# Attention on normalised queries and keys, one core: other homes for the second pair's squares and the early roots, a last pair in three pieces, values loaded one pair later, and new order lists

## The chip, the core and the metric

The kernel runs on one core of one Trainium2 chip. A core has a matrix engine (PE in the profile, with its weight loads as PEld), VectorE (DVE), ScalarE (ACT), GpSimd (POOL) and a sync engine (SP) that issues most transfers. The matrix engine writes its results into the accumulation memory PSUM; everything else lives in the on-chip memory SBUF. The metric is device time in microseconds (us) of one launch; lower is better.

## What is computed

Queries and keys are scaled to length one, their products divided by tau = 0.1, and a softmax over the keys weighs the values. There are 8 x 12 = 96 heads of 512 positions and 64 dimensions.

```python
Q_norm = Q / (np.linalg.norm(Q, axis=-1, keepdims=True) + 1e-10)
K_norm = K / (np.linalg.norm(K, axis=-1, keepdims=True) + 1e-10)
scores = np.einsum('bhqd,bhkd->bhqk', Q_norm, K_norm) / tau
weights = np.exp(scores - np.max(scores, axis=-1, keepdims=True))
weights = weights / (np.sum(weights, axis=-1, keepdims=True) + 1e-10)
return np.einsum('bhqk,bhkd->bhqd', weights, V)
```

Scores lie between -10 and 10 here, so the kernel takes the exponential without the maximum. The row sum comes from a column of ones beside the values.

## The kernel before

The 96 heads are worked off as 48 pairs, s = 0 to 47. One pair passes through these operations; the names in capitals are the keys that the code gives them, and w is 0 for queries and 1 for keys.

- **LD, LV** (L286, L289, L292): SP loads Q, K and V of the pair, 256 KB each. For pair 0, Q and K come in halves of 128 KB, the K halves issued by ACT.
- **SQ** (L227, L229, L306, L308, L313): squares of Q and K. From pair 3 on POOL squares both in one instruction of 128x1024. In pair 1, DVE squares Q (L308) and ACT squares K (L306); in pair 2, ACT squares Q and POOL squares K.
- **SSQ, RED** (L330, L337, L341): sums of squares. Either PE adds eight slices into PSUM with eight products against the identity (SSQ) and DVE finishes the sum (RED, L337), or DVE sums straight from SBUF (L341).
- **LOG, NEW** (L355, L357, L360): one over the root. For pairs 1, 2 and 3 ACT takes a logarithm (LOG) into `ys` and then exp(-x/2) (NEW, kind 7) into `xs` in SBUF, and DVE copies that to PSUM (`nps`, L360; NEW, kind 6). From pair 4 on DVE takes Newton steps. For pair 0 it is done by halves (L236, L240, called NRMS).
- **SCL** (L246, L389): Q and K times their roots, into `qn`. Q is on DVE; K is on POOL, but on DVE for the pairs in `K_ON_DVE` (1, 2, 3, 4, 9, ...).
- **TR, EVA** (L254, L395, L402): PE transposes `qn` into PSUM, DVE copies it out to `qt`.
- **SCO, EXP** (L429, L445): for each of four blocks c of 128 keys PE makes the scores of both heads in `scps`, and ACT writes their exponential to `et`, 128x1024 in one instruction. `scps` holds two such blocks; SCO of block c waits for EXP of block c-2.
- **VC** (L450): POOL turns the values into bf16.
- **PV, RCP, NRM, ST** (L459, L474, L476, L483): PE multiplies `et` with the values, head 0 into bank `ops0` and head 1 into `ops1`; DVE takes one over the row sum (RCP) and scales into `ob` (NRM); SP stores.

In the last pair, 47, block c = 3 is taken by two instructions of 128x512, one for each head, and each head has its own RCP, NRM and store of 128 KB.

The engines run side by side and meet only at semaphores. Nothing is decided at run time: `ORDER` (L525) holds one list per engine, and each engine issues its operations in the order of its list, waiting before each for what it needs (`write`, L67). An operation that waits therefore holds up all that stands behind it on its engine. The PE list also holds fill products on zeros (L188). The first part of the lists, by names:

```
PE   ... TR(0,K,h0) TR(0,Q,h0) SSQ(1,Q) fill TR(0,K,h1) fill fill SSQ(1,K) fill SCO(0,c1,h0) TR(0,Q,h1)
     SCO(0,c0,h0) SSQ(2,Q) SCO(0,c0,h1) SCO(0,c1,h1) SSQ(2,K) SCO(0,c2) TR(1,K) TR(1,Q) SCO(0,c3) SCO(1,c0) ...
ACT  ... NRMS(0,K,h1) NRMS(0,Q,h1) SQ(1,K) SQ(2,Q) LOG(1) EXP(0,c1,h0) NEW(1) EXP(0,c0,h0) EXP(0,c0,h1)
     EXP(0,c1,h1) LOG(2) NEW(2) EXP(0,c2) EXP(0,c3) EXP(1,c0) LOG(3) NEW(3) EXP(1,c1) ... (EXP only from here)
DVE  ... SCL(0,Q,h0) SQ(1,Q) EVA(0,K,h0) EVA(0,Q,h0) RED(1,Q) SCL(0,Q,h1) RED(1,K) EVA(0,K,h1) EVA(0,Q,h1)
     copy(1) RED(2,Q) SCL(1,K) RED(2,K) SCL(1,Q) copy(2) EVA(1) SCL(2,K) SCL(2,Q) RED(3) RED(3) copy(3) EVA(2) ...
```

Of the kernel before, what the change touches and what calls it, by code (L numbers as in the profile page):

```python
# [3 lines left out]
ALU = mybir.AluOpType  # L4
# [102 lines left out]
def bass_cosine_similarity_attention_kernel(  # L107
# [162 lines left out]
    def new(g):  # L270
        if g <= 0:
            return []
        return [("NEW", g, k) for k in (6, 7)]

    def pair(s):
# [6 lines left out]
        for w, x in ((0, Q), (1, K)):  # L282
            if s == 0:
                for h in range(2):
                    P.add(("LD", 0, w, h), "act" if w else "sp", "ldh", -1000 + h,  [],
                          lambda e, w=w, x=x, h=h: e.dma_start(out=qk[iq][:, w, h], in_=src(x, s)[:, h]), slot=f"head{w}_{h}")  # L286
                continue
            P.add(("LD", s, w), "sp", "ld1" if s == 1 else "ld", s, [*([("SCL", 0, w, 0), ("SCL", 0, w, 1), ("SQ", 0, w, 0), ("SQ", 0, w, 1)] if s == R_QK else [key("SCL", s - R_QK, w), key("SQ", s - R_QK, w if s - R_QK in SQ_ON else 0)])],
                  lambda e, w=w, x=x: e.dma_start(out=qk[iq][:, w], in_=src(x, s)),  # L289
                  slot=f"first{s}_{w}" if s <= 2 else f"qk{iq}")  # L290
# [9 lines left out]
        elif s in SQ_ON:  # L300
            for w, eng in enumerate(SQ_ON[s]):
                half, dst = qk[iq][:, w], sq[iqs][:, 8 * w : 8 * w + 8, :]
                half = half.rearrange("p h x -> p (h x)")
                dst = dst.rearrange("p g d -> p (g d)")
                if eng == "act":
                    emit = lambda e, half=half, dst=dst: e.activation(out=dst, in_=half, func=ACT.Square)  # L306
                else:
                    emit = lambda e, half=half, dst=dst: e.tensor_tensor(out=dst, in0=half, in1=half, op=ALU.mult)  # L308
                P.add(("SQ", s, w), eng, {"act": "sqa", "dve": "sqv", "pool": "sqp"}[eng],
                      due_sq(s) + 0.1 * w, [("LD", s, w)] + red[w] + (["table"] if eng == "act" else []), emit)  # L310
        else:
            P.add(("SQ", s, 0), "pool", "sq", due_sq(s), [("LD", s, 0), ("LD", s, 1)] + reds_,
                  lambda e: e.tensor_tensor(out=sqf, in0=data, in1=data, op=ALU.mult))  # L313
# [8 lines left out]
        for w in range(2):  # L322
            sqs = ("SQ", s, w if s in SQ_ON else 0)
            dst = x2[:, w, c8 : c8 + 8]
            if (s, w) in session:
# [9 lines left out]
                P.add(("SSQ", s, w), "pe", "ssq", due, [sqs, "eye"] + before, ssq)  # L335
                P.add(("RED", s, w), "dve", "redp", due + 0.1, [("SSQ", s, w), ("NRMS", 0, 0, 1), *new(g - R_X)],
                      lambda e, bank=bank, dst=dst: e.tensor_reduce(  # L337
                          out=dst, in_=o_ps[bank][:, 320:384].rearrange("p (g e) -> p g e", e=8), axis=AX.X, op=ALU.add))
            else:
                P.add(("RED", s, w), "dve", "red", due_red(s) + 0.5 * w, [sqs, ("NRMS", 0, 0, 1), *new(g - R_X)],  # L340
# [11 lines left out]
        if s == first[g] and g in NORM_ON_ACT:  # L352
# [3 lines left out]
            P.add(("NEW", g, 7), "act", "sm_act", at + 0.01, [("LOG", g)],  # L356
                  lambda e: e.activation(  # L357
                      out=xs[g][:, 0 : 2 * m], in_=ys[g % R_X][:, 0 : 2 * m], func=ACT.Exp, scale=-0.5)).own = True
            P.add(("NEW", g, 6), "dve", "new", TF - 2.6, [("NEW", g, 7), ("NRMS", 0, 0, 1)],
                  lambda e: e.tensor_copy(out=n_ps[:, g % R_X, 128 : 128 + 2 * m], in_=xs[g][:, 0 : 2 * m]))  # L360
# [22 lines left out]
        for w in range(2):  # L383
# [4 lines left out]
                  [("NEW", g, 6 if acts and dve else 6 + w + (dve and w))] + ([("TR", 0, w, 0), ("TR", 0, w, 1)] if s == R_QN else [key("TR", s - R_QN, w)]),  # L388
# [23 lines left out]
    def exps(s, c):  # L412
        if s < 0:
            return []
        if s == NP - 1 and c == NT - 1 or s == 0 and c < 2:
# [3 lines left out]
    def rest(s):  # L419
# [3 lines left out]
        for c in range(NT):  # L423
# [15 lines left out]
            for hs in ((0,), (1,)) if s == 0 and c < 2 or last_pair and c == NT - 1 else ((0, 1),):  # L439
# [13 lines left out]
                  scalar1=1.0, scalar2=1.0, op0=ALU.mult, op1=ALU.mult))  # L453
        for h in range(2):
            for i in range(NT):
                def pv(e, h=h, i=i):
                    for k in range(NT):
                        t, c = (k, i) if last_pair else (i, k)
# [3 lines left out]
                            start=(c == 0 and (t == 0 or not last_pair)), stop=(c == NT - 1),  # L462
                            skip_group_check=last_pair)
# [3 lines left out]
                if last_pair:  # L467
                    need = [("EXP", s, i, h) if i == NT - 1 else ("EXP", s, i)]
                    due = T0 + 0.9 * i + 2.5 + 0.1 * h
# [9 lines left out]
        for h in range(2) if last_pair else (None,):  # L479
            hs = slice(0, 2) if h is None else slice(h, h + 1)  # L480
            P.add(("ST", s) if h is None else ("ST", s, h), "sp", "ld", s + STORE_AT,
                  [("NRM", s, i) for i in range(hs.start, hs.stop)],
                  lambda e, hs=hs: e.dma_start(  # L483
                      out=src(out, s)[:, hs], in_=ob[io][:, hs].rearrange("p h t d -> p h (t d)")),
                  slot=f"out{io}" if h is None else f"outz{h}")
# [6 lines left out]

GROUPS = [1, 1, 1, 1, 2]
SQ_ON = {1: ("dve", "act"), 2: ("act", "pool")}
# [6 lines left out]
VLAG = 3  # L501
# [19 lines left out]
def slack(s, most):  # L521
# [5 lines left out]
        "7 8 64 65 103 104 11 142 143 66 180 181 105 223 224 144 257 258 182 299 300 225 333 334 259 376 377 301 410 "  # L527
        "411 335 452 453 63 378 102 412 141 454 179 222 486 487 528 529 562 563 488 605 606 530 639 640 256 564 681 682 "
        "298 607 715 716 332 641 757 758 375 683 791 792 409 717 834 835 451 759 868 869 485 793 910 911 527 836 944 "
        "945 561 870 986 987 604 912 1020 1021 638 946 1063 1064 680 988 1097 1098 714 1022 1139 1140 756 1065 1173 "  # L530
        "1174 790 1099 1215 1216 833 1141 1249 1250 867 1175 1292 1293 909 1217 1326 1327 943 1251 1368 1369 985 1294 "
        "1402 1403 1019 1328 1444 1445 1062 1370 1478 1479 1096 1404 1521 1522 1138 1446 1555 1556 1172 1480 1597 1598 "
        "1214 1523 1631 1632 1248 1557 1673 1674 1291 1599 1707 1708 1325 1633 1749 1750 1367 1675 1783 1784 1401 1709 "
        "1825 1826 1443 1751 1477 1785 1520 1827 1554 1596 1630 1672 1706 1748 1782 1824 1859 1860 "
    ),
    "pool": (
        "0 1 2 4 14 27 22 35 107 50 145 89 183 226 128 260 209 166 302 232 336 379 243 274 285 308 319 413 396 438 351 "
        "455 362 472 489 531 427 461 565 608 642 503 591 514 537 684 718 580 548 760 794 837 656 625 690 667 871 913 "
        "701 732 766 743 777 947 854 809 820 989 1023 1066 1100 885 930 919 896 1142 1176 961 1006 972 995 1083 1159 "
        "1049 1218 1038 1125 1252 1295 1329 1114 1148 1371 1278 1312 1405 1190 1201 1235 1224 1354 1447 1267 1388 1481 "  # L540
        "1524 1558 1343 1507 1377 1430 1541 1600 1634 1419 1464 1583 1453 1676 1617 1496 1710 1659 1752 1693 1786 1572 "
        "1606 1735 1828 1769 1811 1648 1682 1846 1724 1758 1800 1834 "
    ),
    "dve": (
        "5 13 15 26 28 19 67 24 21 70 32 72 37 34 75 109 78 111 76 114 80 117 115 147 149 152 119 155 184 153 55 186 56 "
        "227 229 61 187 62 188 189 157 190 191 192 100 263 193 194 101 195 196 198 261 200 94 303 305 95 264 139 265 "
        "230 266 140 267 133 234 268 134 269 177 271 270 380 171 339 172 272 337 276 178 382 214 340 306 341 215 342 "
        "220 343 221 344 310 345 347 346 414 349 348 248 416 249 385 353 456 254 458 383 417 255 418 290 419 291 420 "
        "387 421 296 422 297 423 424 425 459 324 492 325 330 490 331 429 532 367 534 368 493 566 494 373 495 374 496 "
        "463 497 609 498 568 401 500 499 402 407 501 408 643 505 535 611 443 569 444 570 449 571 450 572 539 573 685 "  # L550
        "574 477 645 575 576 478 578 577 719 614 483 582 612 687 519 646 484 647 520 648 616 649 761 650 525 651 526 "
        "653 652 553 721 554 654 559 688 795 658 763 560 596 722 838 723 597 724 602 725 603 726 692 727 872 729 630 "
        "797 728 631 730 636 914 764 637 840 734 798 799 678 800 672 801 679 802 673 803 805 804 768 806 712 807 713 "
        "706 874 707 841 948 811 843 990 916 748 875 749 876 877 1024 878 754 879 755 845 880 950 881 882 782 883 783 "
        "788 917 1101 789 887 1067 825 992 826 951 952 831 953 832 954 921 955 956 957 1026 958 859 959 865 860 866 "
        "1177 1143 963 993 901 1069 902 1027 907 1028 908 1029 1030 1031 1032 997 1033 1034 1036 1035 935 1103 936 1070 "
# [90 lines left out]
```

## Time and profile before

| | |
|---|---|
| four runs | 191.6, 191.83, 191.97, 192.09 us; median 191.9 us |
| the profiled execution | 191.83 us, of which the profile's span is 190.1 us |
| granted PE clock in it | 1.0 |
| busy share of the span | PE 93%, ACT 96%, DVE 89%, POOL 81% |
| EXP, all sizes (L445, ACT) | 195 instructions, 176.6 us busy |
| squares from pair 3 on (L313, POOL) | 45 instructions, 84.6 us busy |
| DMA | 267 GB/s mean; 256 KB loads of V land 5.0 us (median) after their issue |

The busy shares are means over three stages with different limits: a head up to the first exponential, a long body, and an end. A busy PE counts overlapping pipelined products. The useful views are the chain of work that ended last, which names at each moment what everything else waited for, and the timeline of one engine, whose last bracket says how long the engine idled before a group of instructions and what ended that. In a timeline a start stamp can lie before the end of the instruction ahead of it, as instructions overlap in the engine's pipe. The prediction shows the lines it rests on.

### The profile page before, as it was taken

The numbers are of one execution on the slowest core, as the hardware profiler recorded it, in microseconds if no ns is written. First come the engines' busy times: TensorE is split into PE (matmuls) and PEld (weight loads), VectorE is DVE, ScalarE is ACT, GpSimd is POOL, SyncE is SP. The second block draws the span as 40 slices with busy tenths as digits, with TensorE's granted clock in tenths as the row PEclk, the third lists the DMA queues.
The fourth block names the chain that finished last, engine by engine and source line by source line (L and its number), as shares of the span: only waits on it lengthen the run. The fifth ranks groups of instructions, "written<-read, shape, count | busy, mean of one in ns | idle before, by whom it ended". The sixth has DMA issues, their size and how long they took to land.

```text
span 190.1 us, 6749 instructions
## 1 busy us (share of the span) xinstructions
PE 176.4 (93%) x2730; PEld 110.8 (58%) x2730; DVE 169.0 (89%) x588; ACT 182.0 (96%) x212; POOL 154.3 (81%) x143
## 2 busy tenths in 40 slices
PE   7889999999999999999999999999999999999983
PEld 2546655656565666656566566665656555655552
DVE  2798999999999999999989999999999888968643
ACT  4599999999999999999999999999999999999993
POOL 5389999999999999999999989979999987043000
PEclk9999999999999999999999999999999999999999
DMA  5999997799999999998798896999699684222133
GB/s 151 356 350 347 349 356 262 221 302 357 380 383 351 316 282 302 382 360 249 247 338 291 263 317 211 345 299 338 217 316 328 193 294 120 62 94 74 55 110 114
DMA packets 52302, 50.76 MB, mean 267 GB/s; under 512 B 3120, under 2 KB 52272, under 8 KB 52272
## 3 DMA queue, kind: packets, MB, share of 16 engines
q1 hardware_dynamic: 51984, 50.08, 81.1%
q8 instruction: 21, 0.34, 0.8%
q10 hardware_dynamic: 288, 0.26, 0.4%
q14 instruction: 9, 0.07, 0.1%
HBM read 37.75 MB, written 12.58 MB: 265 GB/s over the span
## 4 chain that ended last, share of the span: by engine, by line
ACT 92%; DMA 3%; PE 2%; DVE 1%; SPq 0%; ACTq 0%; issue 0%
ACT et L445 92%; DMA qk<-in_Q_dram 3%; PE ops L330 1%; PE scps L429 1%; DVE ob L476 0%; SPq L286 0%; DVE sq L308 0%; ACTq L85 0%; ACT xs L357 0%; ACT ys L355 0%; PE tps L254 0%; PE scps L254 0%; PE ops L459 0%; DVE rd L474 0%; PE scps L188 0%
## 5 line engine op out<-in xcount | busy, mean ns | idle before, releaser
L445 ACT ACTIVATE et<-scps 128x1024 bf16<-128x1024 f32 (+1 forms) x195 | 176.6, 1206 | 0.0
L313 POOL TENSOR_TENSOR sq<-qk 128x1024 bf16<-128x1024 f32 x45 | 84.6, 1893 | 4.0 <-DMA qk<-in_K_dram 3.7
L429 PE MATMUL scps<-qt 64*128 64x512 bf16 x384 | 75.5, 385 | 8.4 <-ACT et L445 2.5
L459 PE MATMUL ops<-vb,et 128*128 128x65 bf16 x1536 | 76.6, 195 | 0.2 <-ACT et L445 0.2
L459 PEld LDWEIGHTS ops<-vb,et 128*128 128x128 bf16 x1536 | 57.6, 98 | 29.6 <-issue 21.1
L389 POOL TENSOR_TENSOR qn<-qk,rk 128x512 bf16<-128x512 f32 x37 | 38.3, 1043 | 11.1 <-DVE rk L367 10.4
L476 DVE TENSOR_TENSOR ob<-ops,rd 128x256 f32<-128x256 f32 x96 | 39.8, 417 | 0.3
L389 DVE TENSOR_TENSOR qn<-qk,nps 128x512 bf16<-128x512 f32 x57 | 38.0, 673 | 0.0
L429 PEld LDWEIGHTS scps<-qt 64*128 64x128 bf16 x384 | 19.6, 93 | 27.1 <-ACT et L445 10.3
L402 DVE COPY qt<-tps 128x1024 bf16<-128x1024 bf16 x47 | 32.2, 685 | 2.6 <-PE tps L395 2.0
L395 PE MATMUL tps<-ident,qn 128*128 128x128 bf16 x376 | 33.8, 220 | 0.1
L450 POOL TENSOR_SCALAR vb<-vf 128x512 bf16<-128x512 f32 x48 | 29.6, 626 | 1.4 <-PE scps L429 1.2
L341 DVE TENSOR_REDUCE nps<-sq 128x8 f32<-128x512 bf16 x44 | 29.8, 680 | 0.0
L395 PEld LDWEIGHTS tps<-ident,qn 128*128 128x128 bf16 x376 | 21.5, 98 | 11.7 <-issue 6.1
L474 DVE RECIPROCAL rd<-ops 128x4 f32<-128x4 f32 x96 | 16.8, 176 | 8.2 <-PE ops L459 5.4
L330 PE MATMUL ops<-sq,ident 128*128 128x64 bf16 x400 | 19.8, 193 | 0.7 <-DVE sq L308 0.7
L330 PEld LDWEIGHTS ops<-sq,ident 128*128 128x128 bf16 x400 | 14.9, 98 | 3.3 <-issue 1.6
L337 DVE TENSOR_REDUCE nps<-ops 128x8 f32<-128x64 f32 x44 | 9.4, 214 | 0.7 <-PE ops L330 0.6
L362 DVE TENSOR_TENSOR nps<-nps,ys 128x32 f32<-128x32 f32 x44 | 8.5, 192 | 0.4
L363 DVE SCALAR_TENSOR_TENSOR nps<-nps,ys 128x32 f32<-128x32 f32 x44 | 8.5, 192 | 0.4
L367 DVE SCALAR_TENSOR_TENSOR nps<-nps,ys 128x16 f32<-128x16 f32 x29 | 5.0, 173 | 0.1
L185 PE MATMUL ops<-warm_in,ident 128*128 128x512 bf16 x8 | 3.6, 631 | 1.4 <-POOL eps L178 1.4
(43 smaller groups left out, 37.5 us busy)
## 6 DMA issues: line engine op xcount, KB each, us to landing
vf<-in_V_dram SPq DMA_DIRECT2D x48, 256.0 KB, 5.0
qk<-in_Q_dram SPq DMA_DIRECT2D x47, 256.0 KB, 4.4
qk<-in_K_dram SPq DMA_DIRECT2D x47, 256.0 KB, 5.6
out_dram<-ob SPq DMA_DIRECT2D x47, 256.0 KB, 4.2
qk<-in_K_dram ACTq DMA_DIRECT2D x2, 128.0 KB, 2.9
qk<-in_Q_dram SPq DMA_DIRECT2D x2, 128.0 KB, 2.7
out_dram<-ob SPq DMA_DIRECT2D x2, 128.0 KB, 1.7
```

What stands on the lines that cost most here:

```text
L313: lambda e: e.tensor_tensor(out=sqf, in0=data, in1=data, op=ALU.mult))
L330: last = e.matmul(out=o_ps[bank][:, 320:384], lhsT=ident[:, :], rhs=sq[iqs][:, 8 * w : 8 * w + 8, 8 * k : 8 * k + 8], start=(k == 0), stop ...
L341: lambda e, w=w, dst=dst: e.tensor_reduce(out=dst, in_=sq[iqs][:, 8 * w : 8 * w + 8, :], axis=AX.X, op=ALU.add))
L389: lambda e, w=w, r=r: e.tensor_tensor(out=qn[iqn][:, w].rearrange("p t h d -> p h t d"), in0=qk[iq][:, w].rearrange("p h (t d) -> p h t d" ...
L395: last = e.transpose(t_ps[:, w, t, :], qn[iqn][:, w, t].rearrange("p h d -> p (h d)"), ident[:, :])
L402: lambda e: e.tensor_copy(out=qt[iqt][:, :, :, :].rearrange("p w t x -> p (w t x)"), in_=t_ps[:, :, :, :].rearrange("p w t x -> p (w t x)")))
L429: last = e.matmul(out=sc_ps[:, 2 * b + h, :], lhsT=qt[iqt][64 * h : 64 * h + 64, 1, c, :], rhs=qt[iqt][64 * h : 64 * h + 64, 0, :, :], sta ...
L445: lambda e, c=c, b=b, hs=hs: e.activation(out=et[iet][:, c, hs[0] : hs[-1] + 1, :], in_=sc_ps[:, 2 * b + hs[0] : 2 * b + hs[-1] + 1, :], f ...
L450: lambda e: e.tensor_scalar(out=vb[:, iq, :, :, 0:DIM].rearrange("p c h d -> p h c d"), in0=vf[iv][:, :, :].rearrange("p h (c d) -> p h c ...
L459: last = e.matmul(out=o_ps[h][:, 65 * t : 65 * t + 65], lhsT=et[iet][:, c, h, 128 * t : 128 * t + 128], rhs=vb[:, iq, c, h, :], start=(c = ...
L474: lambda e, h=h, grid=grid: e.reciprocal(out=rd[io][:, h, :], in_=grid[:, :, DIM]))
L476: lambda e, h=h, grid=grid: e.tensor_tensor(out=ob[io][:, h], in0=grid[:, :, 0:DIM], in1=rd[io][:, h, :].unsqueeze(2).to_broadcast([128, N ...
```

## The change

1. **SQ of pair 1** leaves DVE. Q is squared by ACT (128x512); the K square is split by heads: h0 by ACT (128x256), h1 by POOL (128x256). On ACT's list the Q square stands ahead of NRMS(0,Q,h1), the K square behind it.
2. **Roots of pairs 1 to 3**: ACT's exp(-x/2) writes to `nps` in PSUM; the three DVE copies go. NEW(2) and NEW(3) now stand one EXP behind their LOG. Each NEW also waits for the SCL of the pair before, and sums of pairs 4 to 11 wait for NEW(3).
3. **Last pair**: EXP of block c = 3, PV, RCP, NRM and the store come in three pieces: head 0 whole, head 1 rows 0 and 1, head 1 rows 2 and 3 (`PIECES`). The third piece accumulates in the transposes' PSUM bank. ACT's list has the third piece ahead of the second, PE's and SP's the second ahead of the third; DVE's ends RCP, NRM of piece 1, RCP 2, RCP 3, NRM 2, NRM 3.
4. **VLAG 3 to 4**: V of a pair is loaded one pair later; on SP's list Q and K of pairs 1 to 3 are now followed by V of pair 0 (before: pairs 1 and 2).
5. **All five lists are new**. The PE list's fills differ: 256 columns ahead of SSQ(1,Q), none behind it, one of 256 ahead of SSQ(1,K) (before 256 and 128).

```diff
+    def direct_r(g):
+        return g in NORM_ON_ACT and all(i in K_ON_DVE for i in range(first[g], first[g] + sizes[g]))
...
-            P.add(("NEW", g, 7), "act", "sm_act", at + 0.01, [("LOG", g)],
+            P.add(("NEW", g, 7), "act", "sm_act", at + 0.01, [("LOG", g)] + ([("SCL", first[g] - 1, w) for w in range(2)] if direct and g > 1 else [("NRMS", 0, 0, 1), ("SCL", 0, 0, 1)]),
                   lambda e: e.activation(
-                      out=xs[g][:, 0 : 2 * m], in_=ys[g % R_X][:, 0 : 2 * m], func=ACT.Exp, scale=-0.5)).own = True
-            P.add(("NEW", g, 6), "dve", "new", TF - 2.6, [("NEW", g, 7), ("NRMS", 0, 0, 1)],
-                  lambda e: e.tensor_copy(out=n_ps[:, g % R_X, 128 : 128 + 2 * m], in_=xs[g][:, 0 : 2 * m]))
+                      out=n_ps[:, g % R_X, 128 : 128 + 2 * m] if direct else xs[g][:, 0 : 2 * m],
+                      in_=ys[g % R_X][:, 0 : 2 * m], func=ACT.Exp, scale=-0.5)).own = True
...
+            if last_pair and c == NT - 1:
+                for k, (h, lo, hi) in enumerate(PIECES):
+                    P.add(("EXP", s, c, k), "act", "exp1" if hi - lo == NT else "exph", T0 + 0.9 * c + 0.3 * k,
+                          [("SCO", s, c)] + [key("PV", s - R_ET, i, NT - 1) for i in range(2)],
+                          lambda e, c=c, b=b, h=h, q=slice(128 * lo, 128 * hi): e.activation(
+                              out=et[iet][:, c, h, q], in_=sc_ps[:, 2 * b + h, q], func=ACT.Exp, scale=inv_tau))
...
+    def last(s, T0):
+        iq, iet, io = s % R_QK, s % R_ET, s % R_O
+        spare = t_ps[:, :, :, :].rearrange("p w t x -> p (w t x)").bitcast(f32)
+        for k, (h, lo, hi) in enumerate(PIECES):
+            bank = spare if k == 2 else o_ps[h]
+            for c in range(NT):
...
+                op = P.add(("PV", s, k, c), "pe", "pv" if hi - lo == NT else "pvh", T0 + 0.9 * c + 2.5 + 0.1 * k,
+                           [("EXP", s, c, k) if c == NT - 1 else ("EXP", s, c), ("VC", s)]
+                           + (([("EVA", s)] if k == 2 else bank_free[s, h]) if c == 0 else [("PV", s, k, c - 1)]), pv)
...
+            P.add(("ST", s, k), "sp", "ldh" if hi - lo == NT else "ldq", s + STORE_AT + k, [("NRM", s, k)],
+                  lambda e, h=h, lo=lo, hi=hi: e.dma_start(
+                      out=src(out, s)[:, h, DIM * lo : DIM * hi], in_=ob[io][:, h, lo:hi].rearrange("p t d -> p (t d)")),
+                  slot=f"outz{k}")
...
+PIECES = ((0, 0, 4), (1, 0, 2), (1, 2, 4))
-SQ_ON = {1: ("dve", "act"), 2: ("act", "pool")}
+SQ_ON = {1: ("act", ("act", "pool")), 2: ("act", "pool")}
-VLAG = 3
+VLAG = 4
```

## The prediction

> **What bounds the kernel now.** I read the chain's shares first, then the chain in order of time, then the timelines of ACT, DVE and SP at both ends. The chain's shares, then its pieces (start, length, what):
>
> ```profile
> ACT 92%; DMA 3%; PE 2%; DVE 1%; SPq 0%; ACTq 0%; issue 0%
> ```
> ```profile
> 6.91 0.70 DVE sq L308
> 7.61 0.05 issue
> 7.66 0.41 PE ops L330 x8
> ...
> 10.57 1.08 ACT et L445 x2
> 11.66 0.20 ACT ys L355
> 11.86 0.02 issue
> 11.88 0.22 ACT xs L357
> 12.10 2.74 ACT et L445 x3
> ...
> 15.28 170.48 ACT et L445 x186
> ...
> 186.86 0.42 DVE ob L476
> 187.28 0.12 DVE rd L474
> 187.40 0.02 issue
> 187.42 0.42 DVE ob L476
> ```
>
> The body is 186 exponentials in a row, 170.48 / 186 = 0.917 us each, with no idle between. The change makes none shorter. It can act on the head (DVE's square of Q1, PE's list up to 10.55, LOG and NEW between exponentials) and on the end after the last exponential; in the body it can only do harm.
>
> **Head, the square.** Before, DVE idled for Q1 and then squared, which PE and DVE's own copies (EVA of pair 0) stood behind:
>
> ```profile
> 6.91 0.69 DVE L308 TENSOR_TENSOR sq<-qk 128x512 bf16<-128x512 f32 x1 [1.13 <-DMA qk<-in_Q_dram]
> 7.52 0.41 DVE L267 COPY qt<-scps 64x512 bf16<-64x512 bf16 x1
> ```
>
> - On ACT a 128x512 square takes 0.63 (the rows at 7.62 and 8.35). From the landing at 6.88 it runs 6.91 to 7.54, so SSQ(1,Q) starts at 7.60 instead of 7.66. DVE's copies move into the idle time.
> - The fill of 192 behind it goes (7.90 to 8.07): TR(0,K,h1) starts at 7.84 instead of 8.07. Of two fills one goes (0.055): PE is ready for SSQ(1,K) at 8.17 instead of 8.46.
> - SSQ(1,K) now waits for POOL too. K1 lands at 7.60; POOL starts 0.07 after a landing (9.08 to 9.15); its 128x256 square takes 0.61 (two in the row at 3.63, 1.32 long); PE follows 0.056 later: 7.60 + 0.07 + 0.61 + 0.06 = 8.34. Gain 0.12 instead of 0.29. POOL idled from 6.66 to 9.15, so its next square is not later.
> - From there PE's list is the old one up to the score that EXP(0,c0,h1) waited for: 10.57 becomes 10.45. LOG(1) does not hold it: RED(1,K) ends at 9.01, ACT's square of Q2 at 8.98 as before.
>
> **Head, the roots.** A start-to-start reading of ACT:
>
> ```profile
> 9.15 0.31 ACT L355 ACTIVATE ys<-xs,eps 128x16 f32<-128x16 f32 x1 [0.17 <-DVE xs L337]
> 9.37 0.58 ACT L445 ACTIVATE et<-scps 128x512 bf16<-128x512 f32 x1
> 9.84 0.20 ACT L357 ACTIVATE xs<-ys 128x16 f32<-128x16 f32 x1
> 9.95 1.71 ACT L445 ACTIVATE et<-scps 128x512 bf16<-128x512 f32 x3
> 11.54 0.31 ACT L355 ACTIVATE ys<-xs,eps 128x16 f32<-128x16 f32 x1
> 11.88 0.22 ACT L357 ACTIVATE xs<-ys 128x16 f32<-128x16 f32 x1
> 12.01 2.83 ACT L445 ACTIVATE et<-scps 128x1024 bf16<-128x1024 f32 x3
> ```
>
> LOG(2), NEW(2), EXP one after the other take 12.01 - 11.54 = 0.46: NEW waits for LOG's end. With an EXP between, as pair 1 already has it, they take 0.215 (9.15 to 9.37) and 0.105 (9.84 to 9.95), 0.32. Gain 0.143 for each of pairs 2 and 3, 0.29. The copies (0.11 of DVE time each) are hidden. What a root written to PSUM costs more or less than one to SBUF I take as nothing: pair 0 has both (0.21 to `xs`, 0.16 to `nps`), bounds -0.05 to +0.05 each.
>
> What is late next: with ACT earlier by 0.12 + 0.14, SCO(0,c3) ends at 12.72 - 0.12 = 12.60 and ACT is ready at 12.64, no cover left. LOG(3) needs both RED(3): EVA(1) starts at 12.44 - 0.12 = 12.32, then 0.61 and two SCL of 0.60, so they end at 14.45, ACT may start at 14.49 and is ready at 14.45: 0.04 lost. NEW(3), 0.5 later than before, feeds SCL(3) at 15.83; counted through DVE's list with its rows, EVA(3) ends at 20.47, 0.7 before SCO(3) has to be done, which takes 0.39. That hides it. The added waits hold nothing: each NEW's SCL has ended (SCL(2) at 14.2, NEW(3) at 15.6), and the sums that wait for NEW(3) stand behind SCL(3), which needs it anyway.
>
> Head: 0.12 + 0.29 - 0.04 = **0.37 gained**. Bounds: 0.25 (the square's gain lost) to 0.45 (nothing lost, POOL's 0.06 quicker).
>
> **Body.** Loads: Q and K of pair 3 land one transfer earlier (0.75 us: 9.83 to 10.58 in place of V0), V0 at 11.34 instead of 9.83, taken by POOL at 12.5 behind SQ(3); PV(0) starts at 15.28 in the old timeline. Later on SP's list V goes out behind the store of eight pairs before instead of nine, still some seven pairs ahead of its PV; the one place where POOL may meet it is rival 3. Work ahead of each point in the lists, by rows: ahead of EVA(s) DVE has 0.94 less (0.61 + 3 x 0.11), only for pair 15 0.10 more, where the trace has 1.73 between EVA(15) and its scores. PE's largest work between two score blocks falls from 0.71 to 0.59, with the block's 0.32 under 0.917. POOL is tightest at SCL(20,K): 1.26 more work ahead of it than at the first body squares, against 1.16 of old slack and a start 0.75 earlier, with the deadline 0.37 earlier: 0.28 left. Besides, a late start of ACT by up to 0.25 costs nothing: in the trace an EXP's length grows from 1.01 at 15.19 to 1.28 later, and late starts shorten the next one while ends stay 0.917 apart. I take nothing, bounds 0 (ends without idle leave nothing to gain) and +0.95 (rival 3).
>
> **End.** Here the new parts stand against each other:
>
> ```profile
> 187.31 0.34 SPq L483 DMA_DIRECT2D out_dram<-ob  x1
> ```
> ```profile
> 187.88 0.34 SPq L483 DMA_DIRECT2D out_dram<-ob  x1
> ```
> ```profile
> DMA to landing us min/median/max: 1.7/1.7/1.7
> ```
>
> - ACT: 1024 elements end 0.917 apart, 512 0.490, so 256 cost 0.28; the last exponential ends 0.06 later, at 186.81 (old clock). PE's last products follow at 186.86 and 186.93; DVE is busy with head 0's NRM until it takes the next RCP at 187.20, as before. Hidden.
> - DVE: RCP 187.20, RCP 187.30, NRM 187.42 (0.22 behind its RCP, as at 187.20). Half an NRM: 0.42 for 256 and 0.68 for 512 elements (L389) give 0.29; the second starts 0.21 later and ends at 187.93 instead of 187.85.
> - SP: the second store may go at 187.74, the third at 187.95, but one issue takes 0.345 and the next follows 0.04 later: 188.13 instead of 187.88, **0.25 late**.
> - Landing: 128 KB takes 1.72 from issue. 64 KB is not in this trace. The final transfer ran its 1024-byte packets at 47 ns, 8 on each of 16 engines; 512-byte ones between 27 (the 4-byte ones take 7 to 9, the rest by size) and 47 give 1.57 to 1.72; by 256 KB less 128 KB (2.15 - 1.72), half a step less, 1.51. I take 1.57, by the packets: 189.70 against 189.60.
>
> The Trainium skill ("DMA: Bandwidth & Descriptors", section "Anatomy of one DMA", given for GpSimd's path, while these go from SP) says that a transfer's fixed part, about 2 us, outweighs its bytes, at 436 bytes per ns. That speaks against cutting a store: 64 KB less would save 0.15, and an uncut 128 KB would take 2.3, which the measured 1.72 contradicts. By it the third store would land at 190.28; the sum goes by the rows.
>
> End: **0.10 lost**. Bounds: 0.16 gained (third store issued as soon as its data is there, landing 1.49) to 0.26 lost (1.72).
>
> **Sum.** 191.83 - 0.37 + 0.10 = 191.56 on the profiled execution. That lies 0.07 under the median, 191.9, which would become 191.63. I forecast 191.6.
>
> **Rivals.**
> 1. *The cut store pays.* For: DVE's data is ready 0.18 before SP is, and SP's issue may be shorter for half the bytes (0.372 at 256 KB, 0.345 at 128). Against: halving saved only 0.03. With 0.16 gained and 0.40 in the head: 191.3.
> 2. *The head pays little.* ACT gets ahead, and PE's and DVE's lists, without cover at 12.6 and 14.45, hold it: the square's gain and half of the roots' go. For: 0.04 of cover. Against: DVE has 0.94 less to do. 0.37 becomes 0.1: 191.85.
> 3. *Slower: a late V load holds POOL.* VC(11) now stands ahead of VC(8), VC(10), VC(9) and SQ(12); its load is issued behind ST(3), about 32.3, where it stood behind ST(2), 28.4. POOL reaches it at about 36.2. Loads landed between 2.1 and 6.4 after issue there. At 6.4, 38.7: POOL stalls 2.5, SCL(10,K) comes 1.2 past its slack (0.76 + 0.93 - 0.37 = 1.3), ACT hides 0.25: 0.95 lost, 192.5. It costs from a landing 5.5 after issue on and outweighs the rest from 5.7. Against: loads beside it, issued at 34.8, took 3.1.
>
> **Chances.** Forecast 48%, rival 1 33%, rival 2 9%, rival 3 10%. About 0.2% (0.38 us) is what a measurement of this kernel can tell from no change. Rival 1 and a little of the forecast's lower edge are faster by more: 35%; the rest of the forecast and rival 2 are within: 55%; rival 3 is slower: 10%. Range: down to both best bounds, 191.83 - 0.45 - 0.16 = 191.2, less 0.1 for the runs' spread; up to 191.83 - 0.25 + 0.26 = 191.84 and the 0.26 by which the highest run lies over the profiled one: 191.1 to 192.1. It leaves out rival 3.
>
> **What would show it.** Right: EXP(0,c0,h1) starts near 10.45; pairs 2 and 3 show LOG, EXP, NEW with starts 0.2 and 0.1 apart from what follows; a body of exponentials 0.917 apart; three issues on SP 0.39 apart, the last landing about 1.57 later. Wrong: a gap between exponentials, a POOL wait on V, or a third issue that starts when its NRM ends.

## The result, and the profile after

The changed kernel takes 191.58 us (median of 39 runs, 190.73 to 194.61) against 191.68 us for the kernel before (60 runs on the same chips, 190.72 to 193.1): ratio 0.9993, 95% interval 0.998 to 1.0005. That is no change that this measurement can tell. Four of the 39 runs, 194.03 to 194.61 us at a granted clock of 0.988 to 0.991 (the others have 0.996 or more), are left out of the ratio. The time lies where the forecast put it (191.6), but the terms do not. The profiled execution of the changed kernel took 192.59 us with a span of 190.8, so it is 0.76 slower than the one of before (191.83, span 190.1).

From the page after: the chain's shares, the group of exponentials, POOL's squares, and the last pair's stores (KB each, us from issue to landing).

```profile
ACT 86%; PE 6%; DMA 3%; POOL 2%; issue 1%; DVE 1%; SPq 0%; DVEq 0%; POOLq 0%
...
L469 ACT ACTIVATE et<-scps 128x1024 bf16<-128x1024 f32 (+1 forms) x193 | 176.0, 1210 | 0.7 <-PE scps L446 0.6
L325 POOL TENSOR_TENSOR sq<-qk 128x1024 bf16<-128x1024 f32 x45 | 84.7, 1893 | 3.0 <-DMA qk<-in_K_dram 2.9
...
out_dram<-ob SPq DMA_DIRECT2D x1, 128.0 KB, 1.7
out_dram<-ob SPq DMA_DIRECT2D x2, 64.0 KB, 1.6
```

POOL has a share of the chain now, and the exponentials have 0.7 of idle time ahead of them (the number behind the last bar), where before they had none:

```profile
L445 ACT ACTIVATE et<-scps 128x1024 bf16<-128x1024 f32 (+1 forms) x195 | 176.6, 1206 | 0.0
```

The chain in order of time (start, length, what) says where:

```profile
6.96 0.02 issue
6.98 0.63 ACT sq L317
...
8.48 0.39 PE ops L342 x8
...
10.59 1.08 ACT et L469 x2
11.68 0.19 ACT ys L367
...
15.93 78.84 ACT et L469 x86
...
100.85 1.89 POOL sq L325
102.74 1.01 POOL qn L404
103.75 0.05 issue
103.80 0.40 PE tps L410 x4
104.19 0.34 PE scps L446 x2
104.54 0.02 issue
104.56 80.78 ACT et L469 x88
```

The body is cut in two. Ahead of 104.56 the chain is no longer ACT's own but POOL's: the square of pair 32 (SQ(32)), the K scaling of pair 26 (SCL(26,K)), its transposes, its scores. The exponential at 104.56 ends 1.655 behind the one ahead of it, instead of 0.917: **a gap of 0.74**. POOL's timeline there, with the idle time and its releaser in the bracket:

```profile
97.12 1.90 POOL L325 TENSOR_TENSOR sq<-qk 128x1024 bf16<-128x1024 f32 x1
100.85 1.89 POOL L325 TENSOR_TENSOR sq<-qk 128x1024 bf16<-128x1024 f32 x1 [1.83 <-DMA qk<-in_K_dram]
102.70 1.04 POOL L404 TENSOR_TENSOR qn<-qk,rk 128x512 bf16<-128x512 f32 x1
```

POOL stood for 1.83 us before SQ(32), because K of pair 32, issued at 94.65, landed at 100.78, and SCL(26,K) stands behind it on the new list. (From 94.8 to 100.8 the chain names PE's work, whose last signal came 0.02 before the landing. In e4, below, the same wait ends 0.07 behind the landing with PE's signal 0.34 ahead of it, so the load is what POOL waited for.) The kernel before has SCL(26,K) ahead of SQ(32) and a copy of values between them; there K of pair 32 landed at 98.67 and SQ(32) began at 102.60, so it had 3.9 us to spare:

```profile
99.15 1.89 POOL L313 TENSOR_TENSOR sq<-qk 128x1024 bf16<-128x1024 f32 x1
101.00 1.04 POOL L389 TENSOR_TENSOR qn<-qk,rk 128x512 bf16<-128x512 f32 x1
102.01 0.63 POOL L450 TENSOR_SCALAR vb<-vf 128x512 bf16<-128x512 f32 x1
```

To compare executions I cut each trace into four terms and leave out when the first loads land, which differs by up to 2 us between executions (the landing of Q1 lies between 5.28 and 7.23 in the twelve traces). Term 1 runs from the landing of K1 to the start of EXP(0,c0,h1); term 2 from there to the end of EXP(1,c2), with the roots in it; term 3, the body, to the end of head 0's last exponential; term 4, the end, to the last landing. All in us:

| kernel | K1 to EXP | roots | body | end | median of runs, ratio to before (95%) |
|---|---|---|---|---|---|
| before | 2.98 | 6.53 | 169.15 | 3.34 | |
| after | 2.94 | 6.28 | 169.87 | 3.58 | 191.58, 0.9993 (0.998 to 1.0005) |
| e1 SCL(26,K) ahead of SQ(32) | 3.33 | 6.29 | 169.85 | 3.57 | 192.2, 1.0025 (1.0006 to 1.0043) |
| e2 values as before | 3.68 | 6.29 | 172.97 | 3.57 | 194.48, 1.0164 (1.0135 to 1.0192) |
| e3 two pieces | 2.94 | 6.29 | 169.13 | 3.34 | 191.5, 1.0 (0.9984 to 1.0017) |
| e4 third store on ACT | 2.94 | 6.29 | 170.19 | 3.34 | 191.31, 0.9991 (0.9969 to 1.0013) |
| e6 roots alone | 2.95 | 6.29 | 170.47 | 3.34 | 191.65, 0.9983 (0.9957 to 1.001) |
| e7 square alone | 2.94 | 6.54 | 169.15 | 3.35 | 191.74, 0.9999 (0.9975 to 1.0024) |
| e8 POOL refilled | 2.94 | 6.28 | 169.13 | 3.56 | 191.29, 0.9962 (0.9937 to 0.9988) |
| e9 roots, squares on ACT | 2.83 | 6.29 | 169.24 | 3.34 | 191.16, 0.997 (0.9949 to 0.9991) |
| e10 refilled, store on ACT | 2.94 | 6.29 | 169.13 | 3.34 | 191.18, 0.9982 (0.9965 to 0.9999) |
| e11 as e10, K1 on ACT | 2.84 | 6.29 | 169.13 | 3.35 | 191.07, 0.9962 (0.9945 to 0.9979) |

The terms come from one traced execution each, the medians and ratios from 6 to 39 runs of a kernel. Where K1 lands early (6.47 in e1, 5.98 in e2), term 1 is longer, as PE's own list then sets that start (the chain of both runs through PE alone from 1.41 to the exponential); those two say nothing of the square.

For the change as a whole: term 1 gains 0.04, term 2 gains 0.25, term 4 loses 0.24, and term 3 loses 0.72 in the traced execution. Without the gap the sum would be a gain of 0.05.

### The profile page after: what moved, and what is told of

It reads as the page before. It is cut to its first block, busy times and chain, and to the rows that moved or that the text cites. A ratio compares the mean times of both kernels' runs of the same rounds, so it can differ in the third digit from the quotient of the medians.

```text
span 190.8 us, 6749 instructions
## 1 busy us (share of the span) xinstructions
PE 177.4 (93%) x2729; PEld 110.3 (58%) x2729; DVE 167.9 (88%) x586; ACT 182.4 (96%) x214; POOL 154.9 (81%) x144
## 4 chain that ended last, share of the span: by engine, by line
ACT 86%; PE 6%; DMA 3%; POOL 2%; issue 1%; DVE 1%; SPq 0%; DVEq 0%; POOLq 0%
ACT et L469 86%; DMA qk<-in_Q_dram 3%; PE scps L446 2%; PE ops L486 1%; POOL sq L325 1%; PE ops L342 1%; PE tps L410 1%; POOL qn L404 1%; SPq L296 0%; DVE ob L527 0%; PE ops L514 0%; ACT sq L317 0%; ACT ys L367 0%; DVE rd L525 0%; PE tps L254 0%
## 5 line engine op out<-in xcount | busy, mean ns | idle before, releaser
L486 PEld LDWEIGHTS ops<-vb,et 128*128 128x128 bf16 x1504 | 56.8, 98 | 29.9 <-issue 23.8
L499 DVE TENSOR_TENSOR ob<-ops,rd 128x256 f32<-128x256 f32 x94 | 39.1, 416 | 0.4
L410 PE MATMUL tps<-ident,qn 128*128 128x128 bf16 x376 | 34.5, 220 | 1.0 <-POOL qn L404 0.9
L382 DVE SCALAR_TENSOR_TENSOR nps<-nps,ys 128x16 f32<-128x16 f32 x29 | 4.8, 173 | 0.1
```

The costliest lines, as they stand in the source:

```text
L410: last = e.transpose(t_ps[:, w, t, :], qn[iqn][:, w, t].rearrange("p h d -> p (h d)"), ident[:, :])
L486: last = e.matmul(out=o_ps[h][:, 65 * t : 65 * t + 65], lhsT=et[iet][:, c, h, 128 * t : 128 * t + 128], rhs=vb[:, iq, c, h, :], start=(c = ...
L499: lambda e, h=h, grid=grid: e.tensor_tensor(out=ob[io][:, h], in0=grid[:, :, 0:DIM], in1=rd[io][:, h, :].unsqueeze(2).to_broadcast([128, N ...
```

## The experiments

My theory after the result: the head's gain is taken back by the end, and POOL's new order makes the gap, by standing SQ(32) with a late load ahead of a scaling that is due. The rival: the values' later load makes the K loads late, whatever POOL's order.

**e1, SCL(26,K) ahead of SQ(32) again**

```diff
 POOL  ... SQ(31)
-      SQ(32) SCL(26,K) VC(29) ...
+      SCL(26,K) SQ(32) VC(29) ...
```

> One pair of entries on POOL's list changes places: the scaling SCL(26,K) stands ahead of the square SQ(32), as in the kernel before; all else is the changed kernel. Theory (POOL's order makes the stall): SCL(26,K) no longer waits for K of pair 32 (landed 100.78), the gap of 0.74 between exponentials at 104.6 goes, the body's exponentials end 0.917 apart throughout, the span is 190.8 - 0.74 = 190.1, and the times gather near 191.1, where the quicker half of the changed kernel's runs lies: median 0.3 to 0.5 under the changed kernel's 191.58. Rival (values loaded one pair later make K loads late wherever they are needed): a gap of 0.4 to 1 us stays, at this or another scaling of POOL, and the times stay spread from 191.1 to 192.7.

The gap stayed, 0.72, at another place; the time is 192.2, above the changed kernel's. The theory in this form fell. POOL's timeline of e1, and ACT's at the gap:

```profile
96.60 1.89 POOL L325 TENSOR_TENSOR sq<-qk 128x1024 bf16<-128x1024 f32 x1
100.31 1.04 POOL L404 TENSOR_TENSOR qn<-qk,rk 128x512 bf16<-128x512 f32 x1 [1.83 <-DVE rk L382]
101.31 1.89 POOL L325 TENSOR_TENSOR sq<-qk 128x1024 bf16<-128x1024 f32 x1
```
```profile
111.09 2.86 ACT L469 ACTIVATE et<-scps 128x1024 bf16<-128x1024 f32 x3 [0.61 <-PE scps L446]
```

SCL(26,K) now waits just as long, 1.83, for its factors: DVE's last Newton step for pairs 26 and 27 (`rk`, L382) ends at 100.23. Neither of the two operations could have run at 98.5. POOL lost the time in either order, and three squares and four copies later SCL(28,K) was late instead (109.23), with the gap at 111.09.

**e2, the values loaded as before**

```diff
-VLAG = 4 (SP: ... ST(20) LV(28) LD(32,Q) LD(32,K) ...)
+SP's list of before (... ST(20) LV(29) LD(32,Q) LD(32,K) ...), the other lists as changed
```

> SP's list is that of the kernel before (values one pair earlier again), with the three stores at its end; POOL's, PE's, DVE's and ACT's lists are those of the changed kernel. Theory (POOL's order makes the stall): SQ(32) still stands ahead of SCL(26,K), so some executions still show POOL waiting 1 to 2 us for K of pair 32 there and a gap near 0.7 between exponentials; times as the changed kernel's, 191.1 to 192.3. The head gets the pair-3 loads 0.75 later, without cost. Rival (the values' later load makes the stall): the gap goes, times near 191.1, and no POOL wait over 0.3 us ahead of SCL(26,K).

Both were wrong: the body has three gaps of 3.84 in all (169.13 to 172.97), 194.48 us. Not all of that is POOL's. The first gap, 2.77, is. Then, after PE had stood for 2.79 us, its granted clock was 0.5 from 98.44 to 101.85, in which two products of scores took 0.61 instead of 0.39; the other two gaps, 0.60 and 0.47, are of that stretch. SP's waits ahead of loads of values (us in total, times, longest) in e2, then in the changed kernel:

```profile
SPq L302 <- POOL vb L474: 15.5, 11, 3.3
...
SPq L302 <- POOL sq L325: 1.1, 2, 0.9
```
```profile
SPq L302 <- POOL sq L325: 4.6, 7, 1.7
...
SPq L302 <- POOL vb L474: 1.5, 3, 0.8
...
SPq L302 <- POOL qn L404: 1.2, 2, 0.6
```

and POOL's timeline of e2, with the bracket as above:

```profile
95.03 1.89 POOL L325 TENSOR_TENSOR sq<-qk 128x1024 bf16<-128x1024 f32 x1 [3.81 <-DMA qk<-in_K_dram]
```

SP's load of values waits for a buffer that POOL has to free: 7.3 us in all in the changed kernel, at most 1.7 at a time (9.9 and 2.9 in the kernel before). With values a pair earlier and POOL's copies (VC) at their new places it is 16.6, up to 3.3 at a time, and the K loads that stand behind on SP's list go out late: K of pair 30 at 90.53, landed at 94.96. So the values' later load does not make the gap; POOL's new list needs it. The two parts of the change hang together.

**e8, POOL refilled.** If POOL lost the time because nothing that was ready stood there, two copies of values would fill it.

```diff
 POOL  ... SQ(31)
-      SQ(32) SCL(26,K) VC(29) VC(27) VC(26) SQ(33) ...
+      VC(27) VC(26) SCL(26,K) SQ(32) VC(29) SQ(33) ...
```

> The changed kernel with three entries of POOL's list ahead of SQ(32), as they stand before the change or nearly so: VC(27), VC(26), SCL(26,K), SQ(32). Theory (POOL stands idle for K of pair 32 while work that is ready stands behind it; SCL(26,K) alone could not fill it, because its factors came at 100.16): VC(27) and VC(26) run from 98.5 to 99.7 while K is under way, SCL(26,K) at 100.2, SQ(32) at 101.2 without a wait, SCL(28,K) 1.2 earlier than with SCL(26,K) alone, no gap at 104 nor at 111; body 169.13 instead of 169.86; median 0.3 to 0.5 under the run with SCL(26,K) alone (192.2), so 191.7 or less, and below the changed kernel's where that has the gap. Rival (each re-ordering only moves the gap on): a gap over 0.3 at a later scaling of POOL, time near 192.

```profile
96.05 1.90 POOL L325 TENSOR_TENSOR sq<-qk 128x1024 bf16<-128x1024 f32 x1
97.91 1.21 POOL L474 TENSOR_SCALAR vb<-vf 128x512 bf16<-128x512 f32 x2
100.03 1.04 POOL L404 TENSOR_TENSOR qn<-qk,rk 128x512 bf16<-128x512 f32 x1 [0.90 <-DVE rd L497]
101.03 1.89 POOL L325 TENSOR_TENSOR sq<-qk 128x1024 bf16<-128x1024 f32 x1
```

As the theory had it: the copies run while the load and the factors are under way, SQ(32) follows without a wait, and the body is 169.13 with no gap. The clean comparison is with e1, whose order is the same but for the two copies: SCL(26,K) starts 90.51 behind EXP(0,c0,h1) in both, but SCL(28,K) comes 1.17 earlier here, and the gap of 0.72 is gone.

Against the changed kernel this one trace decides little, because the load came early. Counted from the start of EXP(0,c0,h1), K of pair 32 landed at 90.19 in the changed kernel (gap 0.74), at 90.53 in e4 (gap 1.07), at 88.94 in e3 (none) and at 89.41 here. A line through the first two puts the first gap of the changed list near 89.45, which is an estimate. In e10 below, with the same order on POOL, it landed at 89.70, where by that line the changed list would lose 0.25; e10 has no gap.

191.29 us, ratio 0.9962. None of the 36 runs of e8, e10 and e11, which share this order, is above 192 us; of the changed kernel's 39 it is 12, of e1's 12 it is 8, of the 60 of the kernel before 11. The later form of the theory holds: the gap is POOL's, and it goes when POOL has ready work at that place.

**e3, two pieces**

```diff
-PIECES = ((0, 0, 4), (1, 0, 2), (1, 2, 4))
+PIECES = ((0, 0, 4), (1, 0, 4))
```

> The last pair goes in two pieces again (two exponentials of 512 elements, two RCP and NRM, two stores of 128 KB); all else is the changed kernel. Theory (three pieces lose 0.24 at the end): from the end of EXP(47,3) of head 0 to the last landing 3.34 as in the kernel before, instead of 3.58; the last store's issue follows its NRM at once (0.04). Span 0.24 less for an execution with the same body: 190.8 - 0.24 = 190.6 with the gap, 189.8 without. Rival (the end's loss came from the records of one execution, a store's landing varies by as much): 3.5 to 3.6 stays, span unchanged.

End 3.34, so three pieces lose 0.24, as the theory had it. The traced execution had no gap (K of pair 32 landed at 98.62), which shows that the gap does not come in each execution. The median, 191.5, tells no difference from the changed kernel.

**e4, third store on ACT**

```diff
-            P.add(("ST", s, k), "sp", ...
+            P.add(("ST", s, k), "act" if k == 2 else "sp", ...
```

> The last of the three stores (64 KB) is issued by ACT, which is idle from its last exponential on, instead of SP; all else is the changed kernel. Theory (SP's issues one after the other make the third store late): the third issue starts at the end of its NRM, 188.36 + 0.05 in the changed kernel's times instead of 188.68, so 0.27 earlier, and the last landing is whichever is later, the second's (189.84) or the third's (190.05): from the end of head 0's exponential to the last landing 3.31 instead of 3.58, level with the two-piece end of the kernel before (3.34). Rival (the landing bounds it, two stores in flight share the 16 engines and each gets slower): the third is issued early and lands no earlier than 190.25, a gain under 0.1.

SP's stores of the changed kernel (first and third; the timeline joins the first two, 0.84 long, to one line), then ACT's third store in e4:

```profile
187.79 0.34 SPq L531 DMA_DIRECT2D out_dram<-ob  x1
```
```profile
188.68 0.44 SPq L531 DMA_DIRECT2D out_dram<-ob  x1
```
```profile
188.32 0.35 ACTq L531 DMA_DIRECT2D out_dram<-ob  x1
```

In e4 the last NRM ends at 188.28 and ACT's issue starts 0.03 later; the end is 3.34, so the loss was SP's issues one behind the other. The same 64 KB store takes 0.35 to issue on ACT and 0.44 on SP, where it follows the one ahead by 0.04 to 0.06. The gap was there too, 1.07; the median is 191.31.

**e6, roots alone; e7, square alone.** Both are the kernel before with one part of the head.

```diff
 e6  ACT  LOG(2) -NEW(2) EXP(0,c2) +NEW(2) ... LOG(3) -NEW(3) EXP(1,c1) +NEW(3);  DVE  -copy(1) -copy(2) -copy(3)
 e7  DVE  -SQ(1,Q);  ACT  +SQ(1,Q), SQ(1,K) by half;  POOL  +SQ(1,K,h1);  PE's fills as changed
```

> The kernel before with one part of the change: ScalarE writes the roots of pairs 1, 2 and 3 straight to PSUM, and an exponential stands between LOG and NEW of pairs 2 and 3; DVE's three copies are gone; all lists, the last pair and the values' loads are else those of before. Theory (the roots make the head's gain): from EXP(0,c0,h1)'s start to the end of EXP(1,c2) 6.28 instead of 6.53, so 0.25 to 0.29 gained; the body keeps 169.13 without a gap, since POOL's list is the old one; the end 3.34. Median 191.6 - 0.27 = 191.3, ratio 0.9986. Rival (the body's lists take it back, since ACT gets ahead of POOL's and DVE's lists): a gap over 0.2 in the body, ratio 1.0.

> The kernel before with the other part of the head: pair 1's Q square on ACT, the second half of its K square on POOL, the fills of the changed kernel there; all else as before. Theory (POOL's hand-off eats what the square gives): SSQ(1,K) starts 0.75 to 0.83 after the landing of K1, where POOL's quarter ends 0.68 after it, against 0.86 in the kernel before; where K1 lands late (7.6) EXP(0,c0,h1) starts 2.94 after K1's landing instead of 2.98, a gain of 0.04; where K1 lands early (6.7 or sooner) pair 0's own chain sets the start and the gain is nothing. Rival (the square gives the predicted 0.12): 2.86 after the landing.

Term 2 is 6.29 in e6 and 6.54 in e7: the roots give 0.25, all of the head's gain. Term 1 is 2.95 with DVE's square (e6) and 2.94 with the new one (e7): the square gives nothing. POOL's quarter and PE's sums of it in e7:

```profile
6.84 0.61 POOL L319 TENSOR_TENSOR sq<-qk 128x256 bf16<-128x256 f32 x1 [0.36 <-DMA qk<-in_K_dram]
```
```profile
7.60 0.39 PE L342 MATMUL ops<-sq,ident 128*128 128x64 bf16 x8
```

6.84 and 0.61 make 7.45; PE starts at 7.60, 0.15 behind, and was ready from 7.57 at the latest. In e6 the rival's gap came, 1.33, but not by ACT getting ahead: K of pair 6 landed at 19.33, 9.1 behind its issue, and POOL stood for it.

```profile
19.41 1.89 POOL L325 TENSOR_TENSOR sq<-qk 128x1024 bf16<-128x1024 f32 x1 [1.47 <-DMA qk<-in_K_dram]
```
```profile
22.13 2.85 ACT L469 ACTIVATE et<-scps 128x1024 bf16<-128x1024 f32 x3 [1.23 <-PE scps L446]
```

So the lists of before have a place of this kind too, near pair 6. The single trace of the kernel before does not show it (K of pair 6 landed 7.4 behind its issue there), nor does e9, with the same list on POOL.

**e9, roots and both squares on ACT, all else as before; e10, e8 with the third store on ACT; e11, e10 with K1's square wholly on ACT**

```diff
-SQ_ON = {1: ("act", ("act", "pool")), 2: ("act", "pool")}
+SQ_ON = {1: ("act", "act"), 2: ("act", "pool")}
```

> The kernel before with the roots written to PSUM as in the change and both squares of pair 1 on ACT (no quarter on POOL); POOL's, SP's and DVE's lists, the values' loads and the two-piece end are those of before. Theory: head 10.22 - 0.29 (roots) - 0.10 (SSQ(1,K) 0.06 behind ACT's square, at 8.36 for a K1 that lands at 7.60) = 9.83 after the landing of Q1 where that is late, body 169.13 without a gap, end 3.34: 0.3 to 0.4 under the kernel before, ratio 0.998 to 0.9985. Rival (a body with the old lists can't take an earlier head): a gap in the body of 0.2 or more, ratio 1.0.

> The changed kernel with VC(27), VC(26) and SCL(26,K) ahead of SQ(32) on POOL's list, and the third store issued by ACT. Theory (the two losses are separate and add up): body 169.13 without a gap, end 3.34 instead of 3.57, so 0.23 under the run with the refilled POOL list alone, whose ratio was 0.9962: 0.995, about 190.8 to 191.1. Rival (the end's 0.23 is within what the last landing varies, or the store from ACT costs elsewhere): end 3.5 or more, ratio as without it.

> As the run beside it, and pair 1's K square wholly on ACT (no quarter on POOL). Theory (POOL's hand-off of 0.146 and its start 0.07 after a landing cost the square its gain): SSQ(1,K) 0.71 after the landing of K1 instead of 0.83, EXP(0,c0,h1) 2.83 after it instead of 2.94, where K1 lands later than about 7; nothing where it lands sooner, since pair 0's chain then sets that start. A gain of 0 to 0.11 against the run beside it. Rival (ACT's square, 0.63 for 512 elements in place of 0.42 for 256, holds the square of Q2 and LOG(1)): LOG(1) and EXP(0,c1,h0) up to 0.2 later, a loss of as much.

Term 1 is 2.83 in e9 and 2.84 in e11 against 2.94: a square wholly on ACT gives the 0.10 that the split one did not (PE starts SSQ(1,K) 0.71 behind the landing of K1, not 0.83; the part on the prediction says what makes the difference). In e10 the gap and the end's loss are gone together. Their ratios to before are 0.997, 0.9982 and 0.9962, each with an interval below 1; e11 is the fastest median, 191.07. Term by term, e10 should lie 0.23 under e8. The ratios have e10 above e8, with intervals that overlap, and between e10 and e11 on one chip the medians differ by 0.11: differences of 0.1% are below what these runs can rank.

## Why the prediction was right, and where it was not

The time was right, and its "no change that can be told" too, but by terms of which two were mis-sized and one was missed. A gap between exponentials was named ahead as a sign of being wrong, and it came.

- **The square: 0.12 predicted, 0.04 at most measured.** The term that failed is "POOL ... 7.60 + 0.07 + 0.61 + 0.06 = 8.34". The landing-to-start time (0.07) and the duration (0.61) hold: 7.652, then 7.720 to 8.332. The last step does not: I took 0.056, and PE starts 0.146 behind POOL's square, in all seven traces in which POOL ends last. EXP(0,c0,h1) starts at 10.59, not 10.45; against K1's landing that is 0.04 earlier than before, and e6, with the old square, has 0.03 of it.

  The 0.09 between the two is not POOL's doing. Where PE waits for POOL alone, it follows as fast as behind the others: 0.056 behind SCL(26,K) (103.742 to 103.798), and 0.057 behind SQ(6) in e6 (whose row, shown with e6, ends at 21.30):

```profile
21.36 0.41 PE L342 MATMUL ops<-sq,ident 128*128 128x64 bf16 x8 [1.06 <-POOL sq L325]
```

  But SSQ(1,K) now waits for two engines, ACT and POOL, and the kernel writes one wait for each (`write`; L76 in the changed kernel). In the trace the wait for POOL is an instruction of its own on PE's queue, 8.371 to 8.422, ahead of the weight load at 8.447 and the product at 8.478:

```profile
L76 PEldq EVENT_SEMAPHORE  x1: 51/51/51, 8.4 to 8.4; - x1
```

  The kernel before has the same behind ACT: at 42.909 scores with such a wait of their own start 0.145 behind the exponential that they waited for. So the step that failed is the hand-off of an instruction with two waits, priced by a row with one.
- **The roots: 0.29, less 0.04 at LOG(3), predicted; 0.25 measured.** The sum held, and the pattern that it asked for is in ACT's timeline: the EXP 0.20 and 0.21 behind LOG, and the next 0.12 and 0.11 behind NEW.

```profile
11.56 0.31 ACT L367 ACTIVATE ys<-xs,eps 128x16 f32<-128x16 f32 x1
11.76 1.03 ACT L469 ACTIVATE et<-scps 128x1024 bf16<-128x1024 f32 x1
12.66 0.20 ACT L370 ACTIVATE nps<-ys 128x16 f32<-128x16 f32 x1
12.78 1.94 ACT L469 ACTIVATE et<-scps 128x1024 bf16<-128x1024 f32 x2
14.64 0.31 ACT L367 ACTIVATE ys<-xs,eps 128x16 f32<-128x16 f32 x1
14.85 1.00 ACT L469 ACTIVATE et<-scps 128x1024 bf16<-128x1024 f32 x1
15.75 0.18 ACT L370 ACTIVATE nps<-ys 128x16 f32<-128x16 f32 x1
15.86 2.84 ACT L469 ACTIVATE et<-scps 128x1024 bf16<-128x1024 f32 x3
```

  A root written to PSUM costs no more than one to SBUF (0.20 and 0.18 against 0.22 twice). LOG(3) waited for DVE's sums (they end at 14.61), which cost 0.03 where the sum had 0.04; nothing else of DVE or PE held ACT there, so rival 2 did not come.
- **The body: nothing predicted, bounds 0 to 0.95; 0.72 in the traced execution, nothing in e3.** The step that failed: "POOL is tightest at SCL(20,K)", worked out from work ahead in the lists alone, and the claim of "the one place where POOL may meet" a late load. I looked for a late load of values; the one that came late was a K load, at SQ(32). Rival 3 had the kind of loss right, a late load that holds POOL, and the place and the tensor wrong; that 0.72 is near its 0.95 is chance, as that was worked out from the slack of another scaling. Its form holds too, a landing up to which nothing is lost: counted from EXP(0,c0,h1), SQ(32) began at 89.00 in e3 and cost nothing, at 90.26 here.
- **The end: 0.10 lost predicted, 0.24 measured.** RCP and NRM, and the exponential's 0.06, came as worked out or up to 0.05 earlier. The mis-sized terms are SP's issue of the second store, 0.44 instead of 0.345, and the landing of 64 KB, 1.64 instead of 1.57; the third issue is 0.32 later than the last one before (1.94 against 1.62 behind head 0's exponential), not 0.25. The trace of before had the row that I did not use: a load of values took 0.37 to issue in four of the five places where SP had been waiting, and 0.47 or more in all 43 where it followed another issue at once. Rival 1 is refuted: the cut store costs when SP issues all of it, and with the last piece on ACT (e4) it neither costs nor pays. The Trainium skill ("DMA: Bandwidth & Descriptors", section "Anatomy of one DMA", given for GpSimd's path) speaks against the cut by a transfer's fixed part of about 2 us. An estimate from its figures puts the landing 2.15 behind the issue; the measured 1.64 decides. What the cut cost here was the time of an issue.
- **The sum.** 0.37 - 0.10 was to gain 0.27. In the terms of the traces it is 0.29 - 0.24 = 0.05, and the gap on top in some executions; the medians differ by 0.10, with an interval from 0.38 gained to 0.10 lost. That the centre was hit is luck: it went out from a median of four runs, 191.9, which 60 runs put at 191.68, and a gain that was 0.2 too large made up for it. The range held because errors of this size lie well within it.

What stays open: how often the gap comes. One execution of each kernel is traced, and the landing of the first loads moves an execution by about as much as the gap does. Nor is it shown why K of pair 32 is late. In the DMA view of the changed kernel between 98.3 and 100.8 the queue of loads is all but saturated, and one transfer of instructions lies among them (packets, MB, share of 16 engines):

```profile
q1 hardware_dynamic: 812, 0.78, 95.9%
q8 instruction: 1, 0.02, 2.3%
```

2.3% of 16 engines for 2.5 us is 0.92 us on one engine, and between 98.22 and 100.78 no transfer landed. The Trainium skill ("DMA: Bandwidth & Descriptors", section "Queues, rings and completion order") says that an engine takes turns between its queues only at the end of a packet, which would make the loads' share on that engine wait for all of it. No view here shows the packets of one engine, and e11 has such a transfer there too (0.97 us from 98.54) with landings at 98.39 and 99.72. No run takes the instruction transfer away, so it is not shown to be the cause.

## What to carry to other kernels

A list written out by hand is safe only for the landing times it was made with: at each place where an engine waits for a load, ask what stands behind the wait that is due soon, and put work that is ready in between, as e8's two copies. Count the signals that an instruction waits for, and price a new hand-off by a row with as many; price an issue by the row of one that follows another at once. And cut executions into terms between marks of the trace: here the first loads' landing moved the total by more than each part of the change.

## What the runs showed of the hardware that was not expected

- PE starts 0.056 to 0.057 behind the engine that it waits for, be it ACT (7.610 to 7.666), DVE (7.600 to 7.657 in the kernel before) or POOL (103.742 to 103.798). It starts 0.145 to 0.146 behind where the last signal is one that it awaits in an instruction of its own: POOL's square (8.332 to 8.478, 7.457 to 7.603 in e7, 7.918 to 8.064 in e4), an exponential of ACT (42.764 to 42.909 in the kernel before).
- An issue on SP that follows another at once takes some 0.1 longer: 0.47 against 0.37 for 256 KB of values. 64 KB of output took 0.44 on SP behind another issue and 0.35 on an idle ACT; no run has it on an idle SP.
- 64 KB of output land 1.63 to 1.69 behind the start of the issue, 128 KB 1.72 to 1.75: half the bytes save some 0.1.
- K loads of 256 KB took between 3.3 and 9.1 us from issue to landing in one body (e6), so a list that leaves less than that between a load's issue and its use can have a gap in some executions and none in others.
